# A gated-mixer encoder layer on one core: x packed into the first weight pieces, and a feed-forward in two channel blocks whose down-projection forms seven block products instead of eight in 16 places

## The chip, the cores and the metric

The kernel runs on one core of one Trainium2 chip. TensorE (PE) multiplies matrices into eight PSUM banks of 128 x 512 float32, VectorE (DVE) and ScalarE (ACT) do elementwise work, GpSimd (POOL) and SyncE (SP) mainly issue DMAs. The metric is the device time of one execution in microseconds (us): the median of the runs, 1331.15 us for the kernel before (three runs, 1331.08 to 1331.82). One execution was taken with the hardware profiler; its rows give every duration used below.

## What is computed

One layer over T = 256 tokens with 2048 channels, all in float32:

```
h = RMSNorm(x); P = h @ w_in            # columns: u, v | q, k, v | two gates
y_A = gMLP(u, v)                        # GELU, LayerNorm of v, mixing over 128 positions
y_B = neighbourhood attention(q, k, v)
x2  = x + (sig(gA) * (y_A @ Wb_A) + sig(gB) * (y_B @ Wb_B)) @ w_out
up  = RMSNorm(x2) @ w_up                # 2 x 5504 columns: gate | value
up  = depthwise conv of width 3 over the tokens + bias
x3  = x2 + (silu(gate) * value) @ w_down   # 5504 rows = 43 tiles of 128, 2048 columns
out = RMSNorm(x3)
```

## The kernel before, in words

**Weights as a stream.** All weight matrices are cut into 473 pieces, packed one behind the other in the order of use. A piece is 128 x 1024 floats (512 KB): two tiles of 128 rows by 512 columns. SP loads them in order (L177) into five buffers `wraw`. To reach float32 accuracy with the faster one-pass type fp32r, each piece is split: ACT writes the rounded high part `whi` (L191), DVE the rest `wlo` (L192). Activations are split the same way. A product then takes three matmuls: high x high (L256), low x high (L257), high x low (L258).

**Two kinds of groups.** A "nat" group (v, the gates, the branches, out, down) holds 128 tokens x 128 rows of activations as the stationary operand and streams 512 weight columns; it has two PSUM banks, one for each token block, and a piece takes 12 matmuls. A "ws" group (u, q/k, up) holds 128 x 128 of the weight and streams the tokens, high and low next to each other (L235, 512 columns), then the low part of the weight against the high tokens (L239, 256 columns).

**What sets the order.** The program is written out by hand, piece by piece. `begin(i)` queues what is due at piece i: loads up to piece i + 5 (LOAD_AHEAD), splits up to piece i + 3 (SPLIT_AHEAD, four buffers of `whi`/`wlo`), and then the tasks that were entered for that piece with `at(i, ...)`: the evictions and elementwise steps of earlier groups. Each engine works through its own queue strictly in this order, so a waiting instruction holds back all that stands behind it on its engine.

**Start.** SP loads x, already transposed, in nine DMAs (L300) between the weight pieces. ACT and DVE scale and split it (L352, L359). TensorE does 9 + 8 transposes of the identity (L321, WAKE) beside the first loads. v has two groups of 512 columns. The rows of x (`xs`, two DMAs of 1 MB, L303) come with pieces 10 and 11; their squares (L869) are tasks of pieces 9 to 12, and the GELU of v (L392) needs the norm that comes of them.

**Feed-forward.** 22 "up" groups (two 128-channel tiles f of gate and of value; the last has one) are evicted in `ev_up`: ACT copies half a bank (L746), DVE adds (L748), then conv (L754, L756, L759, L761) for the first channel tile at piece i + 1 and for the second at i + 3, SiLU and product one piece later (L766, L767), split of the activations one later still (L362, L363). When all 43 activation tiles are there, four "down" groups of 512 columns follow, each over all 43 tiles (22 pieces). Their result is added to `x2` (L781) and squared (L782). The last four pieces of the last group are done for one token block and then for the other, so that `finish` (final norm, output DMAs, L806 to L824) of the first block lies beside the products of the second.

`xr` (L698) loads x again for the residual addition of "out" (L706), 512 KB at a time through POOL.

Of the kernel before, what the change touches and what calls it, by code (L numbers as in the profile page):

```python
# [11 lines left out]
OP = mybir.AluOpType  # L12
# [28 lines left out]
LOAD_AHEAD = 5  # L41
SPLIT_AHEAD = 3
WAKE = (9, 8)


def weight_groups():


    g = []

    def add(key, w, row0, nk, *blocks):
        g.append((key, w, row0, nk, blocks))

    def gate(br, j):
        add(("gate", br, j), "w_in", 0, KD, ((GA0, GB0)[br] + j * 512, 512))

    def branch(br, j):
        add(("branch", br, j), "w_branch", br * 1024, 8, (j * 512, 512))

    def qk(j):  # L60
        add(("qk", j), "w_in", 0, KD, (Q0 + j * 256, 256), (K0 + j * 256, 256))

    for j in range(2):
        add(("vg", j), "w_in", 0, KD, (V0 + j * 512, 512))
    for j in range(2):
        add(("u", j), "w_in", 0, KD, (U0 + j * 512, 512))
    for j in range(2):
        add(("va", j), "w_in", 0, KD, (VA0 + j * 512, 512))
        qk(j)
# [14 lines left out]
    for j in range(4):  # L84
        add(("out", j), "w_out", 0, KD, (j * 512, 512))
    for f in range(0, NF, 2):
        nb = min(2, NF - f) * 128
        add(("up", f), "w_up", 0, KD, (f * 128, nb), (DFF + f * 128, nb))
    for j in range(4):
        add(("down", j), "w_down", 0, NF, (j * 512, 512))  # L90
    return g


def weight_pieces():

    out, starts, at = [], {}, 0
    for key, w, row0, nk, blocks in weight_groups():
        starts[key] = len(out)
        cols = sum(n for _, n in blocks)
        per = max(1, BLOCK // cols) if BLOCK % cols == 0 and cols > 256 else 2  # L100
        for k in range(0, nk, per):
            kn = min(per, nk - k)
            out.append((w, row0 + k * 128, kn, blocks, at, kn * cols))
            at += 128 * kn * cols
    return out, starts, at


def packed_weights(arrays):
    import numpy as np

    pieces, _, total = weight_pieces()
    flat = np.empty(total, np.float32)
    for w, r0, kn, blocks, at, n in pieces:
        rows = arrays[w][0, r0:r0 + kn * 128].reshape(kn, 128, -1)
        d = flat[at:at + 128 * n].reshape(128, kn, -1)
        c = 0
        for c0, cn in blocks:
            d[:, :, c:c + cn] = rows[:, :, c0:c0 + cn].transpose(1, 0, 2)
            c += cn
    return flat  # L120
# [3 lines left out]
def trunk_kernel(ctx, tc, x, x_turned, weights, vectors, ln_g, ln_b, w_s_turned, b_s, rpb, norm_final, out):  # L124
# [14 lines left out]
    psum = keep("psum", bufs=8, space=PSUM)  # L139
# [7 lines left out]

    def bank():
        return psum.tile([128, 512], F32, name="bank")


    pieces, starts, _ = weight_pieces()
    counts = {key: nk for key, _, _, nk, _ in weight_groups()}

    raw, split_t = {}, {}
    n_loaded = [0]
    n_split = [0]
    first = {}

    def load_to(n):  # L160
        while n_loaded[0] < min(n, len(pieces)):
            i = n_loaded[0]
            n_loaded[0] += 1
            if i in preload:
                for f in preload[i]:
                    f()
            _, _, kn, _, off, size = pieces[i]
            w = wpool.tile([128, 2, 512], F32, name="wraw", bufs=LOAD_AHEAD)
            cn = size // kn
            parts = range(kn) if i == 0 else [slice(0, kn)]  # L170
            for k in parts:
# [838 lines left out]
```

## Time and profile before

| | |
|---|---|
| median of three runs | 1331.15 us (1331.08 to 1331.82) |
| the profiled execution's own time | 1331.94 us |
| its span, first to last instruction | 1329.9 us, so 2.04 us lie around it |
| granted TensorE clock | 0.997 |
| instructions | 18442 |
| matmuls | 6817 |
| read from HBM | 256.00 MB, 194 GB/s over the span |

The page of the profile lists the busy time of each engine, the span in 40 slices, the DMA queues, the chain of work that ended last, and the costliest groups of instructions by kernel line. A row such as "L192 DVE TENSOR_TENSOR wlo<-wraw,whi ... x459 | 561.8, 1228" says: line 192, on DVE, wrote `wlo` from `wraw` and `whi`, 459 times, 561.8 us in all, 1228 ns each. Durations of neighbours on one engine overlap at their ends, so the distance from one start to the next (here called the pitch) is what work in a row costs.

### The profile page before, as it was taken

Reading aid. Unit: us, or ns where it says so; the run is one execution under the profiler, and the core shown is the slowest. Engines: PE = TensorE matmul, PEld = TensorE weight load, DVE = VectorE, ACT = ScalarE, POOL = GpSimd, SP = SyncE. Lnnn points to the kernel's source line nnn. Section 1 sums busy time; section 2 is a strip of 40 time slices with the busy share of each in tenths; the row PEclk is TensorE's granted clock in tenths of the full one; section 3 lists DMA queues with packets and bytes.
Section 4 is the critical chain, followed back from the end, with each engine's and each line's share of the span. In section 5 each row is a group of like instructions: output and inputs, shape, how many; then the busy total and the mean of one; then the engine's idle time right before and its main releaser. Section 6 shows DMA issues by size and latency. Waiting matters only on the chain.

```text
span 1329.9 us, 18442 instructions
## 1 busy us (share of the span) xinstructions
PE 1317.1 (99%) x6817; PEld 1124.5 (85%) x6817; DVE 868.5 (65%) x1248; ACT 721.8 (54%) x1059; POOL 100.2 (8%) x192
## 2 busy tenths in 40 slices
PE   8999999999999999999999999999999999999997
PEld 6888888888888888888888888888888888888885
DVE  6576667777564545555878787878787875545454
ACT  6755567576444444545656565656565564434342
POOL 0501065430000000000000000000000000000000
PEclk9999999999999999999999999999999999999998
DMA  9856786655666667666666666666666567656662
GB/s 359 280 185 183 212 225 180 202 159 180 187 189 189 193 189 224 206 201 181 188 190 189 191 189 190 189 191 188 191 186 193 164 196 222 211 186 205 190 199 95
DMA packets 77082, 261.40 MB, mean 197 GB/s; under 512 B 9792, under 2 KB 13760, under 8 KB 76736
## 3 DMA queue, kind: packets, MB, share of 16 engines
q1 hardware_dynamic: 72592, 252.40, 61.5%
q0 software_dynamic: 3968, 7.30, 2.4%
q8 instruction: 53, 0.87, 0.3%
q10 hardware_dynamic: 432, 0.53, 0.1%
q14 instruction: 37, 0.30, 0.1%
HBM read 256.00 MB, written 2.10 MB: 194 GB/s over the span
## 4 chain that ended last, share of the span: by engine, by line
PE 98%; DMA 1%; DVE 0%; SPq 0%; ACT 0%; issue 0%; DVEq 0%
PE bank L235 30%; PE bank L256 17%; PE bank L258 17%; PE bank L257 17%; PE bank L239 16%; DMA wraw<-in_weights_dram 1%; PE bank L592 1%; PE bank L642 0%; PE bank L468 0%; PE bank L730 0%; PE bank L688 0%; PE bank L632 0%; SPq L300 0%; DVE x L820 0%; SPq L177 0%; DVE wlo L192 0%
## 5 line engine op out<-in xcount | busy, mean ns | idle before, releaser
L192 DVE TENSOR_TENSOR wlo<-wraw,whi 128x1024 fp32r<-128x1024 f32 (+1 forms) x473 | 571.4, 1212 | 385.1 <-ACT whi L191 371.5
L191 ACT ACTIVATE whi<-wraw 128x1024 fp32r<-128x1024 f32 (+1 forms) x473 | 492.5, 1045 | 395.4 <-PE bank L257 278.2
L235 PE MATMUL bank<-h,whi 128*128 128x512 f32 x1760 | 423.1, 391 | 0.0
L235 PEld LDWEIGHTS bank<-h,whi 128*128 128x128 f32 x1760 | 322.9, 188 | 61.7
L239 PEld LDWEIGHTS bank<-h,wlo 128*128 128x128 f32 x1760 | 226.4, 191 | 9.0
L239 PE MATMUL bank<-h,wlo 128*128 128x256 f32 x1760 | 230.8, 283 | 0.0
L256 PE MATMUL bank<-whi,h 128*128 128x512 f32 x384 | 151.7, 395 | 0.9 <-ACT h L352 0.6
L257 PE MATMUL bank<-whi,h 128*128 128x512 f32 x384 | 150.0, 391 | 0.8 <-DVE h L359 0.8
L258 PE MATMUL bank<-wlo,h 128*128 128x512 f32 x384 | 150.0, 391 | 0.6 <-DVE wlo L192 0.5
L256 PE MATMUL bank<-whi,a 128*128 128x512 f32 x344 | 133.9, 389 | 0.0
L257 PE MATMUL bank<-whi,a 128*128 128x512 f32 x344 | 133.9, 389 | 0.0
L258 PE MATMUL bank<-wlo,a 128*128 128x512 f32 x344 | 133.9, 389 | 0.0
L256 PEld LDWEIGHTS bank<-whi,h 128*128 128x128 f32 x384 | 72.3, 188 | 16.4 <-ACT h L352 1.0
L257 PEld LDWEIGHTS bank<-whi,h 128*128 128x128 f32 x384 | 72.2, 188 | 16.4 <-DVE h L359 2.0
L258 PEld LDWEIGHTS bank<-wlo,h 128*128 128x128 f32 x384 | 72.1, 188 | 16.4 <-DVE wlo L192 1.5
L756 ACT ACTIVATE tc<-ta,vec 128x256 f32<-128x256 f32 x86 | 47.1, 595 | 70.1 <-DVE ta L754 70.1
L257 PEld LDWEIGHTS bank<-whi,a 128*128 128x128 f32 x344 | 64.6, 188 | 13.5
L256 PEld LDWEIGHTS bank<-whi,a 128*128 128x128 f32 x344 | 64.6, 188 | 13.3
L258 PEld LDWEIGHTS bank<-wlo,a 128*128 128x128 f32 x344 | 64.6, 188 | 13.3
L746 ACT ACTIVATE tb<-bank 128x256 f32<-128x256 f32 x86 | 28.3, 384 | 43.0 <-PE bank L235 42.7
L759 DVE SCALAR_TENSOR_TENSOR tc<-ta,vec,tc 128x255 f32<-128x255 f32 x86 | 41.4, 481 | 14.4 <-ACT tc L756 14.4
L959 POOL DMA_DIRECT2D gfin<-in_norm_final_dram x4 | 2.2, 549 | 642.9 <-DVE tc L767 535.5
(141 smaller groups left out, 1093.6 us busy)
## 6 DMA issues: line engine op xcount, KB each, us to landing
wraw<-in_weights_dram SPq DMA_DIRECT2D x459, 512.0 KB, 4.2
wraw<-in_weights_dram SPq DMA_DIRECT2D x14, 256.0 KB, 3.0
xs<-in_x_dram SPq DMA_DIRECT2D x2, 1024.0 KB, 9.0
vw<-va POOLq DMA_DIRECT2D x32, 64.0 KB, 6.2
xr<-in_x_dram POOLq DMA_DIRECT2D x4, 512.0 KB, 5.5
run<-in_rpb_dram POOLq DMA_DIRECT2D x64, 31.2 KB, 3.9
xk<-in_x_turned_dram SPq DMA_DIRECT2D x7, 256.0 KB, 7.8
gfin<-in_norm_final_dram POOLq DMA_DIRECT2D x4, 256.0 KB, 4.9
```

The costliest lines, as they stand in the source:

```text
L191: nc.scalar.activation(h[:, k, :m], w[:, k, :m], AF.Copy)
L192: nc.vector.tensor_sub(l[:, k, :m], w[:, k, :m], h[:, k, :m].bitcast(F32))
L235: nc.tensor.matmul(p, h[:, k - k0, b * 128:(b + 1) * 128], acts(k), start=k == 0, stop=k == nk - 1)
L239: nc.tensor.matmul(p[:, :T], l[:, k - k0, b * 128:(b + 1) * 128], acts(k)[:, 0, :], start=False, stop=False)
L256: nc.tensor.matmul(p, xh, h[:, kk, :m], start=st, stop=False)
L257: nc.tensor.matmul(p, xl, h[:, kk, :m], start=False, stop=False)
L258: nc.tensor.matmul(p, xh, l[:, kk, :m], start=False, stop=sp)
L592: nc.tensor.matmul(o, Q[s][:, c], k.rearrange("p (r c) -> p r c", r=ROWS)[:, :, k0:k0 + UNION], start=n == 0, stop=n == 1)
L746: nc.scalar.activation(t, p[:, T:], AF.Copy)
L756: nc.scalar.activation(v, u, AF.Identity, scale=ck[:, 1, ch:ch + 1], bias=ck[:, 3, ch:ch + 1])
L759: nc.vector.scalar_tensor_tensor(v[:, 1:], u[:, :T - 1], ck[:, 0, ch:ch + 1], v[:, 1:], op0=OP.mult, op1=OP.add)
L959: nc.gpsimd.dma_start(fin["g", j], bass.AP(tensor=norm_final.tensor, offset=norm_final.offset + j * 512, ap=[[0, 128], [1, 512]]))
```

## The change

**Start.** Each of the first 16 pieces holds one row tile: 256 columns of transposed x and the 1024 columns of v behind them (640 KB). The first is loaded in two DMAs (768 and 512 columns). Four buffers `start` hold them. v is one group with four banks (`first_step`), 12 matmuls a piece as before. For piece 0 DVE, not ACT, writes the high part of x; the first four pieces (EARLY) are split in halves of 512 columns. There are 14 identity transposes (WAKE) in one go. The rows of x come with pieces 16 and 17, the other tables with pieces 18 to 22, the squares are tasks of pieces 11 to 14.

**Feed-forward.** The 43 tiles are two blocks, 0 to 21 and 22 to 42. After a block's "up" groups come its "down" groups, two of 1024 columns, with pieces of one tile x 1024 columns (512 KB as before). The partial result of each block is added to `x2`, which now holds x itself before "out" (two DMAs of 1 MB).

**Seven products.** Two tiles (256 channels), two token blocks and two halves of 512 columns make eight block products, 24 matmuls. In the second, fourth, sixth and eighth pair of tiles of each down group (FF_SEVEN; 4 pairs x 2 blocks x 2 column halves = 16) they become seven, of sums of blocks, after Winograd's form of Strassen's scheme: 9 matmuls in the first piece of the pair, 12 in the second. The sums of weights are made by DVE in place in the raw pieces (`sums`), those of activations in `token_sums`. Seven pairs gather in four extra banks, which `combine` adds to `x2` after the last seven pair of a group. Buffers for split pieces are named units, four, and six from "out" on; `prepare` splits up to four pieces ahead if a unit is free. Only one half-size buffer (HALVES) exists for the first block of a pair.

**Banks, end.** Banks are handed out by hand in the order in which they came free. In the last group the last three pieces (LAST) are done bank by bank, the first column half before the second, and `finish` of token block 0 comes one bank (9 matmuls) before that of block 1.

The diff, cut to what the texts speak of:

```diff
-LOAD_AHEAD = 5
-SPLIT_AHEAD = 3
-WAKE = (9, 8)
+AHEAD = 5
+RAW, UNITS, HALVES = 5, (4, 2), 1
+WAKE = 14
+EARLY = 4
+FF_BLOCKS = ((0, 22), (22, 43))
+FF_SEVEN = (1, 3, 5, 7)
+LAST = 3
...
+    add(("vg",), "wide", "w_in", [([k], (("x", T), (V0, 1024))) for k in range(KD)])
...
+            for c0, c1 in ((0, 768), (768, 1280)) if i == 0 else ((0, size),):
+                nc.sync.dma_start(w[:, c0:c1], ...)
...
+    def sums(i):
+        c0, c1 = slice(0, 512), slice(512, 1024)
+        def one():
+            slot = half_free.pop(0)
...
+            r0 = raw[i][0]
+            high(h, r0[:, c0])
+            low(l, r0[:, c0], h)
+            nc.vector.tensor_add(r0[:, c0], r0[:, c0], r0[:, c1])
+        def two():
+            r0, r1 = raw[i][0], raw[i + 1][0]
+            hb, lb = unit((i, "b"))
+            ht, lt = unit((i, "t"))
+            high(hb, r1)
+            nc.vector.tensor_add(r0[:, c1], r0[:, c1], r1[:, c1])
+            high(ht, r0)
+            low(lb, r1, hb)
+            nc.vector.tensor_add(r1[:, c1], r1[:, c1], r0[:, c0])
+            nc.vector.tensor_add(r1[:, c0], r1[:, c0], r1[:, c1])
+            low(lt, r0, ht)
+            raw_done(i)
+        def three():
...
+            h, l = unit((i, "s"))
+            high(h, r1)
+        def four():
...
+            low(l, r1, h)
+            raw_done(i + 1)
...
+    def prepare(n):
+        while queue and queue[0][0] <= n and queue[0][1] <= len(unit_free) and queue[0][2] <= len(half_free):
+            queue.pop(0)[3]()
...
+    def begin(i):
+        cur[0] = i
+        load()
+        prepare(i + AHEAD - 1)
+        run_tasks(i)
...
+        def combine():
+            nu, nv = (fx["p"].tile([128, 512], F32, name=f"comb{n}") for n in range(2))
+            nc.scalar.activation(nu, p(1), AF.Copy)
+            rest(0, 0, nu, OP.add)
+            nc.vector.tensor_sub(nu, nu, p(6))
+            nc.vector.tensor_sub(nv, nu, p(7))
+            rest(0, 1, nu, OP.subtract)
+            rest(0, 1, p(5), OP.add)
+            rest(1, 0, nv, OP.add)
+            rest(1, 1, nv, OP.subtract)
+            rest(1, 1, p(5), OP.add)
+            free(p(1), p(6), p(7), p(5))
...
+            if n in firsts:
...
+                product(1, acts(k, 0), (h, l))
+                product(5, S[0], (ht[:, c0], lt[:, c0]))
+                product(7, S[2], (ht[:, c1], lt[:, c1]))
...
+            elif n - 1 in firsts:
...
+                product(6, S[1], (hs[:, c1], ls[:, c1]))
+                product(2, acts(k + 1, 0), (hb[:, c0], lb[:, c0]))
+                product(3, S[3], (hb[:, c1], lb[:, c1]))
+                product(4, acts(k + 1, 1), (hs[:, c0], ls[:, c0]))
...
+    def token_sums(f, s):
+        nc.vector.tensor_sub(s[:, 0:2, :], f[:, 0:1, :].to_broadcast([128, 2, 128]), f[:, 1:4:2, :])
+        nc.vector.tensor_sub(s[:, 2, :], f[:, 1, :], s[:, 1, :])
+        nc.vector.tensor_sub(s[:, 3, :], f[:, 2, :], s[:, 2, :])
...
-                at(i + (5 if f0 + 3 == NF else 3), lambda: conv(1))
+                at(i + 3, lambda: conv(1))
```

`product` is the three matmuls of one block product; `high` and `low` are the ACT and DVE halves of a split. The four steps of a pair of pieces (i, i + 1) are queued with the plain pieces in this order: `one`, `two`, then around the split of piece i + 2 `three` ahead of it and `four` behind it.

756 lines of the change are left out of this document (466 added, 290 removed).

## The prediction

> **What bounds the kernel now.** First the page: span, engines, and the chain that ended last.
>
> ```profile
> span 1329.9 us, 18442 instructions
> PE 1317.1 (99%) x6817; PEld 1124.5 (85%) x6817; DVE 868.5 (65%) x1248; ACT 721.8 (54%) x1059; POOL 100.2 (8%) x192
> PE 98%; DMA 1%; DVE 0%; SPq 0%; ACT 0%; issue 0%; DVEq 0%
> ```
>
> The chain is 98% TensorE: fewer matmuls shorten the span wherever TensorE doesn't have to wait instead. Next the windows view by stage (its columns: busy us and count of PE, PEld, DVE, ACT, POOL, then granted clock, DMA share, GB/s), and the matmuls of the down stage from the view of the tile `bank`.
>
> ```profile
> 0.00:53.40 53.40, 49.65 (x212) 39.63 (x213) 30.42 (x44) 37.08 (x63) 8.13 (x22) 1.00 0.95 352
> 617.00:1086.60 469.60, 469.60 (x2701) 415.12 (x2700) 360.91 (x591) 274.47 (x423) 0.00 (x0) 1.00 0.62 186
> 1086.60:1320.50 233.90, 233.90 (x1034) 193.76 (x1032) 121.65 (x128) 99.85 (x114) 2.19 (x4) 1.00 0.60 189
> L256 PE MATMUL bank<-whi,a x344: 388/389/393, 1086.8 to 1320.0; 128*128 128x512 f32 x172
> L258 PE MATMUL bank<-wlo,a x344: 388/389/390, 1087.3 to 1320.5; 128*128 128x512 f32 x172
> ```
>
> The 3 x 344 = 1032 matmuls of down start between 1086.8 and 1320.5, so one every 233.7 / 1031 = 0.2267 us; the 389 ns are its length, not its price. A piece of 12 is 2.72 us, one of 9 is 2.04 us. A piece of up is 469.6 / 22 groups (the last is half) / 8 = about 2.78 us. DVE has 23% free in up and 48% in down. The new work falls on DVE, so its own prices come next, from the groups of instructions and from stretches of the timeline in which it works without a break.
>
> ```profile
> L192 DVE TENSOR_TENSOR wlo<-wraw,whi 128x1024 fp32r<-128x1024 f32 x459 | 561.8, 1228 | 372.8 <-ACT whi L191 360.8 <-PE bank L688 6.0 <-PE bank L730 4.4
> L674 DVE TENSOR_TENSOR g<-g,g 128x512 f32<-128x512 f32 x8 | 5.1, 684 | 0.0
> 1053.30 1.64 DVE L748 TENSOR_TENSOR ta<-bank,tb 128x256 f32<-128x256 f32 x4 [1.17 <-ACT tb L746]
> 1055.46 2.36 DVE L192 TENSOR_TENSOR wlo<-wraw,whi 128x1024 fp32r<-128x1024 f32 x2 [0.52 <-ACT whi L191]
> 1057.74 0.76 DVE L754 TENSOR_TENSOR ta<-ta,rb 128x256 f32<-128x256 f32 x2
> 1060.67 1.22 DVE L192 TENSOR_TENSOR wlo<-wraw,whi 128x1024 fp32r<-128x1024 f32 x1
> 516.89 1.29 DVE L674 TENSOR_TENSOR g<-g,g 128x512 f32<-128x512 f32 x2
> 1067.67 0.42 DVE L767 TENSOR_TENSOR tc<-tc 128x256 f32<-128x256 f32 x1
> 1068.01 0.69 DVE L192 TENSOR_TENSOR wlo<-wraw,whi 128x512 fp32r<-128x512 f32 x1
> 1068.61 0.42 DVE L363 TENSOR_TENSOR a<-tc,a 128x256 fp32r<-128x256 f32 x1
> ```
>
> Start to start: two 1024-column lows take 1057.74 - 1055.46 = 2.28, so 1.14 each; a 512 pass 1068.61 - 1068.01 = 0.60 (its duration 0.69); a 256 pass 0.34; a conv 1060.67 - 1057.74 = 2.93 us, with its waits for ACT; the four adds that evict an up group 1.64.
>
> **1. Products saved.** 16 block products less are 48 matmuls: 48 x 0.2267 = **-10.9 us**. The Trainium skill ("TensorE: Matmul & The Clock Gate", the section on 56 against 53.3 ns) gives 215.7 ns for 512 columns; by it the saving is 10.4 us. The trace is at 0.2267.
>
> **2. The start.** The rows: TensorE's idle transposes, ACT's first split, the loads of 6 to 8 us (from a windows view, last number GB/s), the first matmul, one later gap, and the first matmul of u.
>
> ```profile
> 1.38 3.89 PE L321 MATMUL bank<-ident 128*128 128x128 f32 x17 [1.38 <-POOL ident masks.py:199]
> 3.85 0.63 ACT L191 ACTIVATE whi<-wraw 128x512 fp32r<-128x512 f32 x1 [1.16 <-DMA wraw<-in_weights_dram]
> 6.00:8.00 2.00, 0.82 (x3) 1.29 (x3) 1.00 0.87 305
> 4.93 0.79 PE L256 MATMUL bank<-whi,h 128*128 128x512 f32 x1
> 11.43 0.50 PE L258 MATMUL bank<-wlo,h 128*128 128x512 f32 x1 [0.53 <-DVE wlo L192]
> L235 PE MATMUL bank<-h,whi x1760: 386/389/477, 53.7 to 1086.6; 128*128 128x512 f32 x196
> ```
>
> From 4.93 to 53.7 us are 48.8 us for 192 matmuls of v, worth 43.5: 5.2 us are lost in gaps. After: as many bytes (384 KB) are needed first, asked for 0.45 us earlier, and ACT's 0.63 us no longer has x behind it. 14 transposes last 1.38 + 14 x 0.229 = 4.6 us, and I put the first matmul there. Piece 1 makes 1.3 MB in all; with loads flowing from about 2 us on at 280 to 305 GB/s it lands at about 6.7 us, is split to 7.85, and TensorE is done with piece 0 at 7.5: a gap of 0.4. From piece 2 on loads lead. With 0.2 for the first lows, v ends at 4.6 + 0.6 + 43.5 = 48.7, **5.0 us earlier**.
>
> Something is given back. The rows of x leave SP later, for the load of piece 15 ahead of them waits for the buffer of piece 11, which is split when TensorE has finished piece 7: 5.2 + 8 x 2.72 = 27.0, and 2.5 us of splitting. Then 3.3 MB stand in line up to the second megabyte.
>
> ```profile
> 10.00:14.00 4.00, 0.89 (x2) 1.79 (x4) 1.00 1.04 412
> 18.88 0.42 SPq L303 DMA_DIRECT2D xs<-in_x_dram  x1
> 35.65 0.61 ACT L869 ACTIVATE junk<-xs 128x512 f32<-128x512 f32 x1
> 36.39 0.63 ACT L869 ACTIVATE junk<-xs 128x512 f32<-128x512 f32 x1
> 48.83 1.28 ACT L392 ACT_TABLE_LOAD   x1
> 50.12 0.69 ACT L392 ACTIVATE vg<-bank,n_r 128x512 f32<-128x512 f32 x1
> ```
>
> At 412 GB/s that is 8 us: they land near 39.5, while ACT comes to the squares at 36.6 and stands. Behind it: eight squares (0.74 to 0.8 each), four splits, then at the end of v a table (1.28) and four GELUs (0.69). Counted through, piece 19 is split at 57.5 us and wanted at 57.0, since TensorE comes sooner than before. I take 1 us for this, between 0 and 4. Term: **-4.0 us** (-5.0 to -1).
>
> **3. The tail.** Before, the last two evictions stand so:
>
> ```profile
> 1316.16 0.69 DVE L781 TENSOR_TENSOR x<-bank,x 128x512 f32<-128x512 f32 x1 [3.63 <-PE bank L258]
> 1319.95 0.54 DVE L820 TENSOR_SCALAR x<-h,r,e 128x512 f32<-128x512 f32 x1
> 1320.92 0.69 DVE L781 TENSOR_TENSOR x<-bank,x 128x512 f32<-128x512 f32 x1 [0.43 <-PE bank L258]
> ```
>
> `finish` of block 0 holds DVE for 1319.95 + 0.54 - 1316.16 = 4.33 us. Before, 4.76 us of products lay between the two blocks, after only 9 matmuls, 2.04 us: block 1 starts 2.3 us late. **+2.3 us**.
>
> **4. DVE in the seven pairs.** A seven pair costs DVE three 1024 lows, one 512 low and four 512 adds: `one` 1.2, `two` 4.1, `four` 1.14, 6.5 us, against 2.28 for a plain pair; TensorE spends 21 x 0.2267 = 4.76 on it. ACT has 3.5 highs, less. Over plain and seven pair DVE has 8.8 us of work in 10.2: it holds. (The Trainium skill, "VectorE: DVE Perf Modes", section on the 8-slice pipeline, says that float32 with two tensors runs at one element per cycle: 512 at 0.96 GHz are 0.53 us, an estimate; the trace's 0.60 agrees, so no faster mode will rescue the adds.)
>
> But right after up it doesn't hold. The order is strict: with T0 the start of a down group behind up, `one` of the second seven pair (pieces 6, 7) is queued only at piece 3, because the one half-size buffer is free then, and by that time DVE has the evictions of the last up group in front of it. The rows of such an end in the trace, from the chain of waits and ACT's timeline:
>
> ```profile
> 1051.69 3.65 PE bank L235 x16
> 1054.38 2.06 ACT L191 ACTIVATE whi<-wraw 128x1024 fp32r<-128x1024 f32 x2
> wraw<-in_weights_dram SPq DMA_DIRECT2D x459, 512.0 KB, 4.2
> ```
>
> The 16 matmuls are 8 of the group's last piece and 8 of the next group's first, so the group ends at about 1053.5; DVE's adds run from 1053.30 to 1054.94, T0 + 1.44, and ACT's next split starts at T0 + 0.88. Queue of block 0 from T0: the adds, 1.44; lows of piece 4 and of `four`, 2.28; piece 5, 1.14; conv, 2.93; gate, 0.34; `one` and `two`, 5.3; the other conv, 2.93; piece 8 and `four`, 2.28. That sums to 18.6. Product 6 in piece 7 needs `four` by T7 + 0.45 = 7 pieces (5 x 2.72 + 2 x 2.04) + 0.45 = 18.1: 0.5 late from work alone. With DVE's waits for ACT, counted through (1.4 for the highs of `three` and piece 4 behind ACT's four copies, 0.6 for SiLU and the half, 1.0 for `three` and piece 8 behind the conv's ACT part), it is 21.7: 3.6 us late.
>
> Block 1 has a shorter last up group (one channel tile), 11.1 us for 8 pieces, in which the evictions of a full group and the first sums have to fit. From its start on: adds to 1.44; four small lows 2.4; two convs 5.86, two gates 0.68, pieces 0 and 1, 2.28, split 0.6, `one` and `two` 5.3, small eviction 0.67, piece 4 and `four` 2.28: 21.5, that is T0 + 10.4, wanted at T0 + 7.9: 2.5 late from work alone, 2.9 with waits. The next pair adds 2.2 and 3.6. Both together 4.7 to 6.5. From the third seven pair on the lead is back. Sum of the two blocks 5.2 (work alone) to 10.1; some of ACT's waits will lie beside each other, so I take the middle, **+7.5 us**. The two other down groups of a block begin behind down, with only four adds (2.9 us) ahead: no wait.
>
> **At no cost.** The sums of tokens and their split add at most 3 x 0.34 + 0.60 = 1.6 us to the 77% of 22.3 us, 17.1, that DVE works in an up group. `combine` is eight 512 passes and an ACT copy, 6 us, behind four pieces already split (10.9 us); without that lead it would cost 6. x into `x2`: two DMAs of 1 MB on POOL instead of four halves.
>
> ```profile
> xr<-in_x_dram POOLq DMA_DIRECT2D x4, 512.0 KB, 5.5
> 502.95 0.73 POOL L698 DMA_DIRECT2D xr<-in_x_dram  x1 [213.13 <-PE bank L258]
> 538.23 1.40 DVE L706 TENSOR_TENSOR x<-bank,xr 128x512 f32<-128x512 f32 x2
> ```
>
> 35 us lie between issue and use, and 512 KB took 5.5 us to land. Pieces of one tile by 1024 columns have the same bytes.
>
> **Sum.** -10.9 - 4.0 + 2.3 + 7.5 = -5.1 us. Profiled execution 1331.94 to 1326.8; the median lies 0.8 lower, so **1326.1 us** (-0.4%).
>
> **Rivals.** *The lead covers it* (DVE's lateness vanishes in buffers): for it, 372.8 us of DVE's idle time over the span stand ahead of its lows; against it, the strict order above. -10.9 - 4.0 + 2.3 = -12.6, **1318.5 us**.
>
> *Nothing left:* lateness at its upper 10.1 and the start held to -1 by the GELU queue: -10.9 - 1 + 2.3 + 10.1 = +0.5, **1331.7 us**. For it: ACT is busy 37.08 of the first 53.4 us already.
>
> *Slower: DVE becomes the bound of the seven pairs.* If passes cost their durations (1228, 690, 684 ns) instead of the pitch, because sums in place each wait for the pass before, and every pair begins 0.75 us late (ACT's half-size high first), a plain and a seven pair take 7.1 + 2.5 + 0.75 = 10.3 us, over TensorE's 10.2, the point from which it decides. A further 0.5 comes if the second raw piece, whose buffer is free at the end of `two`, 3.9 us before the next pair begins, takes the 4.2 us to land that the row shows. Then the lead never returns: 12 further pairs at 0.1 to 0.6, 4 us, and the queues above with durations for pitches 4.7 + 9.1 = 14: -10.9 - 4.0 + 2.3 + 14 + 4 = +5.4, **1336.5 us**. Against it: the pitches are measured on lines of the same kind.
>
> The Trainium skill ("TensorE: Matmul & The Clock Gate", Part 1) says that some 3.4 us of idle array halve the clock; a single wait of that length would then cost about 1.7 us more (an estimate). No row here shows it: the granted clock is 1.00 over the first 53.4 us, with gaps of about half a microsecond such as the one quoted.
>
> **Chances.** Forecast 0.5, cover 0.25, nothing left 0.13, slower 0.12. A measurement of this kernel tells 0.2%, 2.7 us: faster means below 1328.5. The forecast's own range, 1322 to 1330.5, lies four fifths below that: faster 0.25 + 0.40 = 0.65; same 0.10 + 0.12 = 0.22; slower 0.13. Range 1318 to 1333.5: it takes in cover, forecast and nothing left, and leaves out the slower rival and the far ends.
>
> **What would show it.** 48 matmuls fewer; first u matmul near 49 us; in the down stages gaps of TensorE only at the first and second seven pair behind up, released by DVE lows of the sums; down groups behind down at 2.72 and 2.04 us a piece without gaps; last eviction 2.3 us later behind the last matmul. Wrong if gaps stand at every seven pair (slower rival), at none (cover), or in up.

## The result, and the profile after

The changed kernel takes 1345.88 us (median of four runs, 1344.24 to 1347.45) against 1331.49 us for the kernel before beside it: ratio 1.0108, 95% interval 1.0091 to 1.0126. It is 14 us slower where 5 us faster was forecast, and lies outside the range. The profiled execution took 1345.03 us. Below, one of the five executions of e4, which ran at a granted clock of 0.556 (2211.84 us), is left out of its time and ratio.

The page of the profile after (span, engines, chain by engine):

```profile
span 1342.9 us, 18498 instructions
PE 1312.0 (98%) x6766; PEld 1117.6 (83%) x6766; DVE 966.9 (72%) x1397; ACT 736.0 (55%) x1082; POOL 96.5 (7%) x190
PE 91%; DVE 4%; ACT 2%; issue 1%; DMA 1%; SPq 0%; DVEq 0%; ACTq 0%
```

The products are saved as said: 6817 matmuls less 48 of the products, and three transposes fewer at the start, make 6766. But TensorE's share of the chain fell from 98% to 91%, so it now waits. For what, the waits view of TensorE says (line waited at, what released it: us in total, times, longest):

```profile
PE bank L383 <- DVE wlo L247: 11.9, 7, 2.6
PE bank L381 <- ACT whi L244: 2.9, 1, 2.9
PE bank L372 <- DVE wlo L247: 2.3, 1, 2.3
```

L383 and L381 are products of down, L372 is a product of u: nine waits in these three rows, none of them in up (what else the view lists lies in the first 10 us). Where they stand, and what else happened there, shows the windows view of after (same columns as before; the value ahead of the DMA share is the granted clock):

```profile
57.00:61.00 4.00, 1.72 (x12) 1.44 (x11) 1.48 (x2) 3.43 (x8) 3.41 (x7) 1.00 0.35 60
61.00:65.00 4.00, 4.00 (x15) 3.42 (x15) 1.30 (x3) 2.53 (x6) 3.81 (x12) 0.57 0.78 224
872.00:876.00 4.00, 1.37 (x5) 0.84 (x6) 3.53 (x5) 2.49 (x4) 0.00 (x0) 1.00 0.20 75
1226.00:1230.00 4.00, 2.79 (x12) 1.73 (x10) 3.30 (x5) 2.77 (x4) 0.00 (x0) 1.00 0.15 29
1275.00:1279.00 4.00, 1.08 (x5) 0.48 (x3) 2.05 (x4) 2.42 (x6) 0.00 (x0) 1.00 0.00 0
1279.00:1283.00 4.00, 1.37 (x4) 0.84 (x5) 2.95 (x3) 3.97 (x6) 0.00 (x0) 0.62 0.21 40
1283.00:1287.00 4.00, 4.00 (x11) 3.13 (x10) 3.90 (x6) 1.90 (x2) 0.00 (x0) 0.52 0.86 304
```

A full 4 us of down holds 17 or 18 matmuls, one of u 23 or 24; the third row has 5, the fifth 5. The second and the last row show another loss: TensorE is busy all 4 us and does only 15 and 11 matmuls, because its granted clock is 0.57 and 0.52. A wait stands ahead of it each time. The matmuls of down are then 0.43 us apart instead of 0.2267.

Laid side by side by stage, with the first matmul of each as marks (u; `va`, the group behind u; up; down), the 13.0 us of longer span are:

| | predicted | measured |
|---|---|---|
| 48 matmuls | -10.9 | -10.9 |
| start, up to the first matmul of `va` (100.00 to 101.10) | -4.0 (-5 to -1) | +1.1 |
| waits in the down groups behind up | +7.5 (5.2 to 10.1) | +11.8 |
| the last down group, behind down | 0 | +8.3 |
| tail | +2.3 | +2.7 |
| up | 0 | 0.0 |
| sum | -5.1 | +13.0 |

The 11.8 are six waits, 4.0 us in block 0 and 6.3 in block 1, and 1.5 us of shorter gaps beside them. The 8.3 are 6.2 us of waits and short gaps and 2.1 of matmuls at half the clock. Of the 18.1 us between forecast and result the last group has 8.3, the start 5.1, the groups behind up 4.3 and the tail 0.4.

**The start.** u begins 3.6 us sooner (50.03 against 53.67). ACT and DVE of after, from their timelines (us, length, engine, line, and in brackets the idle time ahead and its releaser):

```profile
38.41 0.63 ACT L1163 ACTIVATE junk<-xs 128x512 f32<-128x512 f32 x1 [1.17 <-DMA xs<-in_x_dram]
42.61 0.63 ACT L1163 ACTIVATE junk<-xs 128x512 f32<-128x512 f32 x1 [3.48 <-DMA xs<-in_x_dram]
58.42 2.01 ACT L244 ACTIVATE whi<-wraw 128x1024 fp32r<-128x1024 f32 x2
59.52 2.36 DVE L247 TENSOR_TENSOR wlo<-wraw,whi 128x1024 fp32r<-128x1024 f32 x2 [5.13 <-ACT whi L244]
```

ACT stands twice for the rows of x (the second megabyte came at 42.6, not at 39.5), so the norm, the GELU and the splits behind it end late: the high of piece 19 begins at 58.42, its low at 59.52. TensorE stood from 58.4 to 60.8 and then ran 3.4 us at half the clock. Gained 3.6, lost 4.7: 2.4 of wait, 1.8 of half clock, and 0.5 for four transposes of the norm's result. In the kernel before these lay inside v (L344, at 50.5), now they lie inside u (L595, at 65.3), so 0.5 of the 3.6 us is only moved.

**The last group.** DVE and ACT at the change from the first to the second down group of block 1:

```profile
1270.15 0.68 DVE L969 TENSOR_TENSOR x<-bank,x 128x512 f32<-128x512 f32 x1
1271.62 0.69 DVE L1089 TENSOR_TENSOR x<-x,h 128x512 f32<-128x512 f32 x1 [0.79 <-ACT junk L1074]
1272.23 0.68 DVE L969 TENSOR_TENSOR x<-bank,x 128x512 f32<-128x512 f32 x1
1273.77 0.69 DVE L1089 TENSOR_TENSOR x<-x,h 128x512 f32<-128x512 f32 x1 [0.85 <-ACT junk L1074]
...
1278.05 0.69 DVE L1089 TENSOR_TENSOR x<-x,h 128x512 f32<-128x512 f32 x1 [0.85 <-ACT junk L1074]
1279.95 3.69 DVE L247 TENSOR_TENSOR wlo<-wraw,whi 128x1024 fp32r<-128x1024 f32 x3 [1.20 <-ACT whi L244]
```

In the last block the result is final, so the eviction doesn't only add (L969): ACT squares the sum (L1074) and DVE multiplies it by the weight of the final norm (L1089), one behind the other, four times. DVE is held from 1270.15 to 1278.7, 8.6 us, of which the four adds, all that the prediction counted (at 2.9), are 2.7. What is left of the splits of the new group stands behind that. TensorE waits in its first seven pair, for the high of `three` until 1279.02 and for the low of `four`, which stands behind the plain piece's low, until 1282.36.

**The tail.** The evictions of the last two banks in DVE's timeline of after, where the last matmul began at 1330.82:

```profile
1329.62 0.68 DVE L969 TENSOR_TENSOR x<-bank,x 128x512 f32<-128x512 f32 x1
1333.91 0.68 DVE L969 TENSOR_TENSOR x<-bank,x 128x512 f32<-128x512 f32 x1
```

The last eviction starts 3.09 us behind the last matmul, before 0.42: +2.7, and 1333.91 - 1329.62 = 4.29 us is the `finish` of the other block, as the prediction had it.

### The profile page after: what moved, and what is told of

The parts are those of the page before. It is cut to its first block, busy times and chain, and to the rows that moved or that the text cites. A ratio compares the mean times of both kernels' runs of the same rounds, so it can differ in the third digit from the quotient of the medians.

```text
span 1342.9 us, 18498 instructions
## 1 busy us (share of the span) xinstructions
PE 1312.0 (98%) x6766; PEld 1117.6 (83%) x6766; DVE 966.9 (72%) x1397; ACT 736.0 (55%) x1082; POOL 96.5 (7%) x190
## 4 chain that ended last, share of the span: by engine, by line
PE 91%; DVE 4%; ACT 2%; issue 1%; DMA 1%; SPq 0%; DVEq 0%; ACTq 0%
PE bank L366 29%; PE bank L372 15%; PE bank L383 14%; PE bank L381 14%; PE bank L382 14%; DVE wlo L247 2%; PE bank L398 1%; PE bank L401 1%; PE bank L399 1%; ACT whi L244 1%; PE bank L835 1%; DMA start<-in_weights_dram 0%; DMA wraw<-in_weights_dram 0%; ACT junk L1074 0%; DVE x L969 0%
## 5 line engine op out<-in xcount | busy, mean ns | idle before, releaser
L244 ACT ACTIVATE whi<-wraw 128x1024 fp32r<-128x1024 f32 (+1 forms) x470 | 484.2, 1046 | 273.7 <-PE bank L382 151.6
L372 PEld LDWEIGHTS bank<-h,wlo 128*128 128x128 f32 x1760 | 226.8, 191 | 11.5 <-DVE wlo L247 2.5
L372 PE MATMUL bank<-h,wlo 128*128 128x256 f32 x1760 | 231.4, 284 | 2.3 <-DVE wlo L247 2.3
L383 PE MATMUL bank<-wlo,a 128*128 128x512 f32 x312 | 123.4, 396 | 11.9 <-DVE wlo L247 11.9
L381 PE MATMUL bank<-whi,h 128*128 128x512 f32 x320 | 126.0, 394 | 0.0
L381 PE MATMUL bank<-whi,a 128*128 128x512 f32 x312 | 122.8, 393 | 3.1 <-ACT whi L244 2.9
L383 PE MATMUL bank<-wlo,h 128*128 128x512 f32 x320 | 124.8, 390 | 0.0
L382 PE MATMUL bank<-whi,h 128*128 128x512 f32 x320 | 124.7, 390 | 0.0
L382 PE MATMUL bank<-whi,a 128*128 128x512 f32 x312 | 122.2, 392 | 0.0
L701 DVE TENSOR_TENSOR ta<-bank,tb 128x256 f32<-128x256 f32 x110 | 39.0, 416 | 64.1 <-ACT tb L699 64.1
L699 ACT ACTIVATE tb<-bank 128x256 f32<-128x256 f32 x110 | 36.2, 384 | 89.1 <-PE bank L366 83.3
L383 PEld LDWEIGHTS bank<-wlo,a 128*128 128x128 f32 x312 | 59.1, 189 | 27.5 <-DVE wlo L247 15.4
L381 PEld LDWEIGHTS bank<-whi,a 128*128 128x128 f32 x312 | 59.2, 190 | 16.2 <-ACT whi L244 3.9
L383 PEld LDWEIGHTS bank<-wlo,h 128*128 128x128 f32 x320 | 60.1, 188 | 12.7
L381 PEld LDWEIGHTS bank<-whi,h 128*128 128x128 f32 x320 | 60.2, 188 | 12.2
L382 PEld LDWEIGHTS bank<-whi,h 128*128 128x128 f32 x320 | 60.2, 188 | 11.9
L382 PEld LDWEIGHTS bank<-whi,a 128*128 128x128 f32 x312 | 59.1, 189 | 12.3
L1028 DVE SCALAR_TENSOR_TENSOR tc<-ta,vec,tc 128x255 f32<-128x255 f32 x86 | 41.4, 481 | 14.4 <-ACT tc L1025 14.4
```

The lines of the kernel that those rows point to most:

```text
L244: nc.scalar.activation(h, w, AF.Copy)
L372: nc.tensor.matmul(p[:, :T], l[:, c:c + 128], acts(2 * n + k)[:, 0, :], start=False, stop=False)
L381: nc.tensor.matmul(p, xh, wh, start=start, stop=False)
L382: nc.tensor.matmul(p, xl, wh, start=False, stop=False)
L383: nc.tensor.matmul(p, xh, wl, start=False, stop=stop)
L699: nc.scalar.activation(t, p[:, T:], AF.Copy)
```

## The experiments

The theory to be tested: four places, each with its own cause (the rows of x at the start, the final norm at the last change of groups, the pile of sums and evictions behind up, and `finish`). The rivals: that the seven products are themselves too dear for DVE at every pair, or that the half clock has another cause than the waits.

**e1: only the adds at the last change of groups**; square and product become tasks of four later pieces of the next group.

```diff
-            add_down(p, t, q)
-            v = rs["x2"][:, t, q * 512:(q + 1) * 512]
-            nc.vector.tensor_mul(v, v, fin["g", q])
+            v = add_rest(p, t, q)
+            def rest(): ...                # Square on ACT, tensor_mul on DVE
+            if q < 2:
+                at(i + 5 + 4 * (2 * t + c), rest)
...
```

> Edit: where the last channel block's first down group ends, VectorE only does the four adds; the square (ScalarE) and the product with the norm weight of each 128x512 part are tasks of pieces 5, 9, 13 and 17 of the next group. Theory (the chain add, square, product, four times, 8 us long on VectorE and ScalarE, holds back the splits of the next group; TensorE waits 5.9 us there and its clock then runs at half for 6.8 us): the waits of 3.1 and 2.8 us at 1276 to 1282 and the half clock behind them vanish, 9.3 us in all: about 1336.5. Rival (the group's start is late because the loads are late behind the eight passes that add up the seven-product banks, so that the order of add, square and product is innocent): most of the wait stays, 1343 or more.

Measured 1338.24 us (ratio 1.0051, 1.0036 to 1.0066), 7.6 less than after. Windows of e1:

```profile
61.00:65.00 4.00, 3.75 (x14) 3.27 (x15) 1.75 (x4) 2.09 (x5) 3.88 (x11) 0.61 0.81 223
1262.00:1290.00 28.00, 28.00 (x125) 23.21 (x124) 26.66 (x32) 15.58 (x19) 0.00 (x0) 1.00 0.61 196
```

The second row holds the change of groups: 125 matmuls in 28 us, full clock, no wait. So the serial norm at that place was a cause of this term (e4 below shows that it isn't enough alone). Of the 8.3 us 1.2 are left, most of it a wait of 0.9 at 1317 for a low that stands behind `combine`. The start is as bad as in after.

**e2: the rows of x two and four pieces sooner.** **e3: 24 transposes of the identity in the wait at piece 19**, which do nothing but keep TensorE busy.

```diff
-        preload[16 + t] = [lambda t=t: load_rows(t)]
+        preload[12 + 2 * t] = [lambda t=t: load_rows(t)]      # e2
+    at(19, fill)                                              # e3: 24 transposes into a free bank
```

> Edit: the two 1 MB loads of the rows of x go out ahead of pieces 12 and 14 instead of 16 and 17. Theory (ScalarE stands for the rows at 39 to 43 us, everything behind is late, and at piece 19 TensorE waits 2.4 us for the low part of its weights, after which its clock runs at half for 3.4 us): the rows land before 36, the wait and the half clock vanish, u to the first value group keeps its 46.3 us, 4 to 4.7 us less: about 1341.5. Rival (ScalarE simply has too much to do between the squares and the GELU): the wait at piece 19 shrinks by under 1 us and the time stays within 1 us of 1345.9.

> Edit: 24 identity transposes (2.6 us) stand on TensorE ahead of the products of piece 19, where it waits 2.4 us for VectorE. Theory (the half clock from 61 to 65 us follows from TensorE standing idle): the wait is filled, the granted clock stays 1.00 from 57 to 66 us, and u ends 1.5 us earlier although the transposes are extra work. Rival (the clock drops for another reason, such as the time since the start): half clock as before, u ends at the same time or later.

e2 took 1343.88 us (1.0093, 1.0078 to 1.0108), 2.0 less than after where 4 to 4.7 were expected; e3 took 1345.38 (1.0105, 1.0085 to 1.0126; two executions). Windows of e3:

```profile
57.00:61.00 4.00, 4.00 (x35) 3.86 (x33) 0.00 (x0) 3.99 (x11) 2.21 (x6) 1.00 0.57 163
61.00:65.00 4.00, 2.89 (x18) 2.42 (x17) 2.88 (x4) 1.87 (x4) 3.90 (x9) 1.00 0.73 154
```

With TensorE kept busy the clock stays at 1.00 through the stretch where after has 0.57: the idle time takes the clock, nothing else that happens there. It brought no time, for the wait behind the transposes lasted to 62.3 and u ended 1.6 us later. In e2 the first wait shrank from 2.4 to 0.9 us and its half clock went, but 1.2 us of wait appeared at 82.8. ACT no longer stood for the rows, but three times 2.6 us for the value pieces behind them, and its last square ended only 1.5 us sooner (49.1 against 50.7). And this happened 800 us further on, in the windows view of e2:

```profile
868.00:872.00 4.00, 3.10 (x13) 1.93 (x11) 3.12 (x8) 3.60 (x6) 0.00 (x0) 1.00 0.43 131
872.00:876.00 4.00, 2.16 (x5) 1.78 (x6) 4.00 (x6) 2.49 (x4) 0.00 (x0) 0.60 0.57 160
876.00:880.00 4.00, 4.00 (x11) 3.09 (x11) 3.86 (x6) 1.30 (x2) 0.00 (x0) 0.54 0.58 234
```

It is the same wait behind up, 2.78 us, that after shows at 872 to 876 with the clock at 1.00; begun 1.5 us sooner, it is followed by half the clock. The Trainium skill ("TensorE: Matmul & The Clock Gate", Part 1) says that the gate judges windows of about 3.4 us that run freely, and halves the clock behind an idle one. The lengths of 3.4 and 6.8 us, and that the same wait costs differently by where it falls, agree with it; that the window must be idle throughout does not: a wait of 2.4 us (after, at piece 19) and one of 2.78 (e2) were enough here. Which share of a window is enough is not settled by these runs.

**e4: eight products everywhere**, the rest of the change kept.

```diff
-FF_SEVEN = (1, 3, 5, 7)
+FF_SEVEN = ()
```

> Edit: no seven-product pairs; two channel blocks, 1024-column down pieces, start and end as in the changed kernel. 48 matmuls more, 10.9 us. Theory (the work of the sums on VectorE makes the waits behind up, 4.0 and 6.3 us, and is half of the lateness at the last group): these waits vanish too and the last group's mostly, so about 1345.9 + 10.9 - 10.3 - 6 to 9 = 1337.5 to 1340.5, faster than the changed kernel. Rival (the two blocks and the wide pieces cost, the seven products only save): 1345.9 + 10.9 = 1356.8.

1336.62 us (median of four; 1.0039, 1.0023 to 1.0055): 9.3 us faster than after with 48 more matmuls. There is no wait in down at all, so the seven pairs have a part in all waits there, those at the last change too: this kernel does the norm as serially as after, and with plain pairs the lead hides it. The start (`va` at 103.4, a wait of 4.3 us and half the clock) and the tail (12.1 us from last matmul to end, before 9.4) remain: 3.4 + 2.7 = 6.1 us, by which its span (1336.0) is longer than that of before.

**e5: the seven pairs one pair later**, on top of e1. **e6: rows ahead of pieces 8 and 10, their squares and norm two pieces sooner**, on top of e1. **e7: three of the four sums of weights on GpSimd**, on top of e1. **e8: e1, e5 and e6 together.**

```diff
+FF_SEVEN = (2, 4, 6, 8)                                       # e5, e8
+        preload[8 + 2 * t] = [lambda t=t: load_rows(t)]       # e6, e8
+        at(9 + c, lambda c=c: x_stats(c))                     # e6, e8 (was 11 + c)
+    at(13, x_norm)                                            # e6, e8 (was 15)
+            nc.gpsimd.tensor_add(...)                         # e7, three adds per pair
```

> Edit: e1 with the seven-product pairs at the third, fifth, seventh and ninth pair of a group instead of the second, fourth, sixth and eighth. Theory (behind up VectorE still has the evictions of the last up group in front of the sums; two plain pieces more give it 5.4 us): the waits behind up, 4.0 us in the first block and 6.3 us in the second, shrink to 1 to 3 us together, 7 to 9 us less: about 1330. Rival (the waits stand wherever the first two pairs stand, since a pair costs VectorE more than TensorE): as e1, 1338, the waits only two pieces later.

> Edit: e1 with the rows of x ahead of pieces 8 and 10, their squares as tasks of pieces 9 to 12 and the norm of piece 13, each two pieces earlier. Theory (ScalarE's lateness at piece 19 comes of the rows and squares): no wait of TensorE between 50 and 90 us, no half clock, first value group at about 96.5 instead of 101.5, 4.5 to 5 us less than e1: 1333.5. Rival (what is loaded earlier makes the value pieces late): gaps between 25 and 45 us take it back, 1337 to 1338.

> Edit: e1 with three of the four adds of each seven-product pair on GpSimd. Theory (the waits behind up are VectorE's work): 1.9 us less per pair on VectorE take most of the 10 us of waits away, 1330 to 1333. Rival (the adds in a row, each waiting for the last, are the chain, and GpSimd takes 1 us or more for one): the waits stay or grow and new ones stand at the later pairs, 1340 to 1350.

> Edit: e1, e5 and e6 together: adds first at the last transition, later pairs, rows and squares earlier. Theory (the three waits are separate): 48 matmuls saved, -10.9, start -3.6 to -4, what is left of the waits behind up +1 to +3, tail +2.7: 1331.4 - 10 = 1320 to 1323, faster than the kernel before. Rival (the waits are one lateness that moves on when it is removed at one place): 1328 or more.

e6 took 1333.74 us (1.0019, 1.0010 to 1.0028), 4.5 less than e1: no wait between 50 and 90 us, and `va` at 97.1, 2.9 us sooner than before. So the rows of x and their squares together were the cause at the start; e2 had moved the rows but left their squares where they were.

e5 took 1337.35 us (1.0042, 1.0026 to 1.0059), 0.9 less than e1 (their executions overlap), e8 1332.41 (1.0006, 0.9997 to 1.0015), 1.3 less than e6. The waits behind up fell from 10.3 to 6.6 us, where 1 to 3 were expected; half the clock followed one of them (6.8 us of it in e5, 3.4 in e8), and the tail grew to 14.4 and 15.0 us, since `combine` of the last seven pair now stands right ahead of the last evictions. Moving the pairs away from the evictions doesn't cure the waits, as it should have if the evictions were all.

e7 took 1377.22 us (1.0345, 1.0330 to 1.0361). Groups of e7 by line:

```profile
L303 POOL TENSOR_TENSOR wraw<-wraw,wraw 128x512 f32<-128x512 f32 x16 | 36.7, 2291 | 31.9 <-issue 23.9 <-DVE wlo L247 6.0 <-DMA wraw<-in_weights_dram 2.0
L304 POOL TENSOR_TENSOR wraw<-wraw 128x512 f32<-128x512 f32 x16 | 20.7, 1296 | 1.3
```

An add that takes DVE 0.69 us takes GpSimd 1.3, and 2.3 at L303, which begins while DVE's lows still run. The sums are a chain, and from the half-size low of one seven pair to that of the next are 13.2 us (930.42 to 943.61), so waits stand at most pairs, and 37.6 us at half the clock follow them in six stretches: with both the time is 27 us above the rival's 1350.

**e9: the conv of the last up groups put behind the sums**, on top of e6: the shortest way to clear the pile, if it is a pile.

```diff
-            at(i + 1, lambda: conv(0))
+            d0, d1 = {20: (5, 9), 40: (1, 13), 42: (9, 0)}.get(f0, (1, 3))
+            at(i + d0, lambda: conv(0))
             if n > 1:
-                at(i + 3, lambda: conv(1))
+                at(i + d1, lambda: conv(1))
```

> Edit: e6 with the conv steps of the last up groups of a block moved back: group 20 to pieces 5 and 9 of the down group, the second channel tile of group 40 and the one of group 42 to pieces 5 and 9. Pairs as in the changed kernel, the second, fourth, sixth and eighth. Theory (the waits of 4.0 and 6.3 us behind up come from the conv passes, 2.9 us each, that stand in VectorE's queue ahead of the sums; the pairs alone fit): under 2 us of them is left, 8 to 9 us less than e6: 1325 to 1326, faster than the kernel before by 0.4%. Rival (two pieces of 9 and 12 matmuls with 6.5 us of sums cannot be kept up behind any eviction, so the waits only move back): 1331 to 1334.

1335.90 us (1.0033, 1.0020 to 1.0045), 2.2 more than e6 where 8 to 9 less were expected. The waits only moved to the next pairs and became nine (11.9 us in all against 10.0 in seven in e6 by the waits view): once DVE is late, the pairs that follow are late too. That asks for the price of a pair when nothing else is on DVE. Its timeline in e6, from the half-size low of one seven pair towards that of the next:

```profile
877.93 1.22 DVE L247 TENSOR_TENSOR wlo<-wraw,whi 128x1024 fp32r<-128x1024 f32 x1
880.43 3.50 DVE L247 TENSOR_TENSOR wlo<-wraw,whi 128x1024 fp32r<-128x1024 f32 x3 [1.29 <-ACT whi L244]
883.85 0.69 DVE L247 TENSOR_TENSOR half_lo<-wraw,half_hi 128x512 fp32r<-128x512 f32 x1
```

and ACT's there:

```profile
878.39 2.96 ACT L244 ACTIVATE whi<-wraw 128x1024 fp32r<-128x1024 f32 x3 [1.82 <-DVE wraw L304]
```

DVE's last sum is done at 878.0, and ACT's highs may begin. The order in the queue is `three` (a high on ACT), the plain piece (high on ACT, low on DVE), `four` (low on DVE). So the next low on DVE is that of the plain piece, and it needs ACT's second high: DVE stands 1.29 us here and 1.00 in the cycle behind it. From 873.29, where the half-size low before it began, to 883.85 are 10.56 us; TensorE's plain and seven pair are 45 matmuls, 10.2 us.

**e10: e6 with eight products.**

```diff
-FF_SEVEN = (1, 3, 5, 7)
+FF_SEVEN = ()
```

> Edit: e6 without seven-product pairs (eight products everywhere). Theory: no waits behind up, start 3.1 us shorter than the kernel before, tail 2.7 us longer, no clock loss: within 1 us of 1331.4. Beside e9 it gives what the seven products are worth once nothing waits for them (10.9 by the matmuls). Rival (the start's and the rows' repair already took all there is, and the pairs bring nothing): e9 and e10 alike.

1331.52 us (1.0001, 0.9992 to 1.0010), no wait from 10 us on: the start mended (3.5 us won by `va`) and the tail (2.8 lost) nearly cancel. Against it e6's seven products cost 2.2 us though they save 10.9.

**e11: the low of the last sum straight behind its high**, on top of e6. The plain piece goes behind `four`, so that ACT's high of the last sum lies beside DVE's low of the sum before.

```diff
             if late:
                 queue.append((i, 1, 0, late[0]))
-            queue.append((i, 1, 0, split_piece(i)))
-            if late:
                 queue.append((i, 0, 0, late[1]))
+            queue.append((i, 1, 0, split_piece(i)))
```

> As e6 (rows of x and squares early, only the adds of the last down change at the change), and in the queue of splits the low of a pair's last sum (step four) comes straight behind its high (step three), ahead of the split of the next plain piece instead of behind it. Theory (the handover is a part of the price): in a cycle of a plain and a seven pair VectorE's adds take 5.79 us, then it stands 1.0 us for the second of two ScalarE highs, and the three lows take 3.4, 10.2 to 10.3 us against TensorE's 10.2, so that a lead which the queue behind up has used is not won back; with the new order the last sum's high lies beside the low of the sum before it, the 1.0 us goes, and the sum that TensorE waits for is split a further 1.14 us sooner. The 10.3 us of waits behind up then fall to 4 or less, and e6's 1333.7 to 1327 or 1328, below the kernel before. Rival (the waits behind up come only from the evictions of up that stand ahead of the sums, and the order within a pair does not matter): 8 to 10 us of waits stay and the time is 1333 to 1334. A second rival (the plain piece behind the pair is now the late one): the waits stand at the high x low matmuls of plain pieces, with the same sum, 1333 or more.

1327.48 us (0.9968, 0.9956 to 0.9979): 6.3 less than e6 and faster than the kernel before. DVE's timeline in e11 over the same cycle:

```profile
871.78 0.69 DVE L247 TENSOR_TENSOR half_lo<-wraw,half_hi 128x512 fp32r<-128x512 f32 x1
872.50 0.69 DVE L293 TENSOR_TENSOR wraw<-wraw 128x512 f32<-128x512 f32 x1
873.22 0.69 DVE L300 TENSOR_TENSOR wraw<-wraw,wraw 128x512 f32<-128x512 f32 x1
873.83 1.22 DVE L247 TENSOR_TENSOR wlo<-wraw,whi 128x1024 fp32r<-128x1024 f32 x1
875.08 0.69 DVE L303 TENSOR_TENSOR wraw<-wraw,wraw 128x512 f32<-128x512 f32 x1
875.81 0.69 DVE L304 TENSOR_TENSOR wraw<-wraw 128x512 f32<-128x512 f32 x1
876.42 1.22 DVE L247 TENSOR_TENSOR wlo<-wraw,whi 128x1024 fp32r<-128x1024 f32 x1
877.96 3.50 DVE L247 TENSOR_TENSOR wlo<-wraw,whi 128x1024 fp32r<-128x1024 f32 x3 [0.33 <-ACT whi L244]
881.38 0.68 DVE L247 TENSOR_TENSOR half_lo<-wraw,half_hi 128x512 fp32r<-128x512 f32 x1
```

The stand is 0.33 us and the cycle 881.38 - 871.78 = 9.60: 0.6 under TensorE's 10.2 where it was 0.4 over. The exchange also splits the last sum one low sooner; this run doesn't tell the two effects apart. Of the 10.3 us of waits behind up 4.3 are left, 0.5 in block 0 and 3.8 in block 1, and half the clock for about 3 us behind the last of them.

**e12: the first seven pair of the down group behind up in block 1 done as two plain pieces**, on top of e11 (that pair of activations keeps its four plain tiles beside the sums).

```diff
-            seven.update({starts[key] + 2 * p: p for p in FF_SEVEN})
+            seven.update({starts[key] + 2 * p: p for p in FF_SEVEN if (n, j, p) != (1, 0, 1)})
...
```

> As e11, and in the group of block 1 that stands behind up the first of the four seven pairs is done as two plain pieces (three matmuls more; for that pair of tiles the split keeps the four blocks of activations beside the four sums). Theory (what is still waited for behind up in block 1 is the pile of two seven pairs on VectorE within the first eight pieces, beside the evictions of the short last up group): the 4.2 us of waits at 1205 to 1221 us go or fall below 1 us, three matmuls cost 0.7, and the time is 3 us below e11, 1324 to 1325. Rival (the evictions alone hold VectorE back, and the half-size buffer lets the first seven pair be prepared no sooner): the waits only move to the next pair, 3 to 4 us stay, and the time is e11's 1327.5 or up to 0.7 more.

1322.35 us (0.9932, 0.9918 to 0.9945), 5.1 less than e11 for three more matmuls: more than expected. The spans of the profiled executions differ by 6.2: the waits, 3.8; shorter gaps beside them, 0.7; the half clock behind them, 1.5, which the expectation had left out; 0.9 at the start, where the second piece landed later in e11's; less 0.7 for the matmuls. The waits view of e12 for TensorE:

```profile
PE bank L570 <- POOL ident masks.py:199: 1.4, 1, 1.4
PE bank L382 <- DVE wlo L247: 0.4, 1, 0.4
PE bank L397 <- ACT whi L244: 0.2, 1, 0.2
```

One wait of half a microsecond is left in down. The 10.2 us by which its span (1319.7) is under that of before can be read off term by term: 45 matmuls -10.2, `va` at 96.2 -3.8, the wait in down and the short gaps around it +1.0, up 0.0, tail +2.8, which makes -10.2. e12 is the fastest version here; its tail was left as it is.

| | us | ratio to before (95%) |
|---|---|---|
| after | 1345.88 | 1.0108 (1.0091 to 1.0126) |
| e1, norm out of the change of groups | 1338.24 | 1.0051 (1.0036 to 1.0066) |
| e6, and rows and squares of x sooner | 1333.74 | 1.0019 (1.0010 to 1.0028) |
| e11, and `four` ahead of the plain piece | 1327.48 | 0.9968 (0.9956 to 0.9979) |
| e12, and one seven pair plain | 1322.35 | 0.9932 (0.9918 to 0.9945) |

## Why the prediction was wrong

**Products saved: right.** -10.9 us, and e12's ledger closes with 0.2267 us a matmul.

**The start: wrong in size and sign.** v did end 3.6 us sooner (5.0 forecast; the first matmul began at 5.01, not 4.6, and v lost 1.5 us in gaps instead of 0.6); 0.5 of it were transposes that moved into u. The failed step is "I take 1 us for this, between 0 and 4". The chain was named rightly (rows of x, squares, GELU, split of piece 19), but the rows were put at 39.5 us and came at 42.6, and nothing was taken for the clock: 2.4 us of wait and 1.8 of half clock, and the 0.5 of the transposes, in place of 1. "No row here shows it" kept the halved clock out of the sum, and it was wrong. The last stretch of before, behind the final matmul, shows it in the windows view:

```profile
1320.50:1329.90 9.40, 0.39 (x2) 0.00 (x0) 3.85 (x11) 1.65 (x4) 0.00 (x0) 0.65 0.59 211
```

The last matmul ends at 1320.89, and from 1323.3 on the granted clock is 0.50. That kernel has no wait longer than 0.6 us from its first product to its last, so the trace couldn't show how short a wait is enough, but it did show the clock at half 2.4 us after TensorE's last work. e6 gives the term its value without the chain: -2.9.

**The tail: right**, +2.7 for +2.3, by the mechanism named.

**Behind up: the place right in block 1, the cause half.** Worked through with DVE's waits the prediction had 3.6 us in block 0 and 6.5 in block 1; measured were 4.0 and 6.3. In block 1 they stand at the two pairs named, 3.1 and 3.3 us for 2.9 and 3.6. In block 0 the match is partly luck: the pair named waited 2.8 us, and "From the third seven pair on the lead is back" failed, for the third pair waited 1.2. Taking the middle of the two ends was the error of size, since the waits came out at the upper end; 1.5 us of shorter gaps beside them were not in it. The reason is in the ledger "Over plain and seven pair DVE has 8.8 us of work in 10.2: it holds". The passes alone take 9.3 (the sums that wait for the sum before are 0.72 us apart, not 0.60), and the order of the handover adds 1.0 to 1.3. The cycle is 10.3 to 10.6, at or over TensorE's. That is in part the "slower" rival's mechanism, and the reason given against it ("the pitches are measured on lines of the same kind") was no reason: the lines were of the same kind, but independent of each other. The rival's price of 10.3 is partly luck: it let every pass cost its duration (9.6 us) and took 0.75 for a late half-size high, where the passes took 9.3 and the stand is at another handover, that of the last sum. It was wrong about where the price shows: groups that start with a lead of split pieces live on it through four pairs and show no gap (the second down group of block 0). e11 shows how much of the loss hung on the order: 6.3 us for one exchange of two steps.

**The last group: missed.** "The two other down groups of a block begin behind down, with only four adds (2.9 us) ahead: no wait" is the dearest failed step, 8.3 us. It holds in block 0. In block 1 the same eviction also squares and scales for the final norm, a chain over DVE and ACT of 2.14 us a bank. The kernel before does both there too, the square in L782 and the product in L791; the description of it leaves the product out. Its groups on DVE by line:

```profile
L781 DVE TENSOR_TENSOR x<-bank,x 128x512 f32<-128x512 f32 x8 | 5.2, 685 | 4.1 <-PE bank L258 4.1
L791 DVE TENSOR_TENSOR x<-x,gfin 128x512 f32<-128x512 f32 x6 | 4.2, 693 | 0.8 <-ACT junk L782 0.6
```

It adds both banks first and then multiplies both, so DVE stood only 0.8 us over all six products; after goes bank by bank, and DVE stands about 0.85 us for the square each time. The prediction counted only the adds, and not the chain between the two engines. e1 removed it and won 7.6 us. That the wait needs the seven pairs as well, e4 shows.

**No cost in up: right**, 480.1 us in both kernels.

So of the named rivals none came about as a whole: after is slower than the slower rival (1336.5), because three terms went wrong the same way and each brought the halved clock or a further wait with it. With the four edits of the table the kernel comes to 1322.35, between the forecast and the rival in which the lead covers everything.

## What to carry to other kernels

When work on TensorE is traded for work on another engine, count the cycle of that engine with its dependences and its handovers, in the order of the queue, and not the sum of its passes: here 8.8 us of passes were 10.3 to 10.6 us of cycle, and one exchange in the order gave 6.3 us back. An engine that holds on average lives on its lead, so look at each change of stage for what stands in its queue there, chains over two engines above all. A wait of 2 to 3 us of TensorE can cost its own length and nearly as much again in clock (2.78 us and 2.7 behind it in e2), so a sum with such waits needs a term for it.

## What was not expected of the hardware

The granted clock fell to half for 3.4 or 6.8 us behind waits of 2.0 (e11) to 4.3 us (e4) in a stream that was otherwise dense. The same 2.78 us wait did or did not bring it, by when the matmul ahead of it began (872.4 us in after: clock 1.00; 870.8 in e2: 0.54). In e9 waits of 1.4 and 1.9 us with 1.7 us of products between them (887.6 to 892.6) left it at 1.00. Transposes that fill the wait keep the clock at 1.00 (e3).

Sums of 512 columns on DVE that each have to wait for the pass before start 0.72 to 0.73 us behind it (e11); a pass that doesn't follows after 0.61. On GpSimd the same sum took 1.29 us, and 2.29 where it began at 934.46 beside lows of DVE that end at 935.61 (e7): 1.15 + 1.29 would be 2.44, so GpSimd seems to stand until DVE is done. The Trainium skill ("SBUF — State Buffer", "SBUF: two separate sides") has the two engines share a port under an exclusive lock, which would explain it; no run here tells it from another cause.
